# Last output projection of an attention/mLSTM step: one pass per half of the tokens, the norm weight in the last product, Ln from PSUM, and instruction orders stated anew

## The chip, the core and the metric

The kernel runs on one core of one Trainium2 chip. The metric is the device time of one execution in microseconds (us). Before the change the median of three runs is 1099.15 us (1096.28 to 1099.74). A profile of one further execution, which took 1096.84 us, gives the durations used below; its span from the first to the last instruction is 1095.1 us.

The core has five instruction streams: PE (TensorE, matrix products and transposes), DVE (VectorE), ACT (ScalarE), POOL (GpSimd) and SP (SyncE, which here issues most DMAs). Each works through its own list in order; between the lists there are semaphores, so an instruction whose input is not ready holds up all that stand behind it in its list.

## The reference

One inference step of two layers, for 512 tokens of a prompt and 8 sample tokens (520 columns in all), model width 1024, in float32:

```python
x = x + NSA(rmsnorm(x, w_norm0))      # layer 0: native sparse attention, out = W_o(mix * silu(z))
x = x + mLSTM(rmsnorm(x, w_norm1))    # layer 1: matrix-memory LSTM,      out = W_out(h * silu(z))
y = rmsnorm(x, w_norm2)               # final norm, returned for prompt and samples

def rmsnorm(x, w):
    y = x * rsqrt(mean(x * x, axis=-1) + 1e-6)
    return y * w
```

Besides `y` the step returns the new cache rows, the conv rows and the mLSTM's states: per sample a 512 x 512 matrix `C` for each of 4 heads, which are read from HBM, updated and written back.

## The kernel before

**Layout.** `x` is held transposed: 8 tiles of 128 features by 520 tokens. The tokens are worked on in two halves of `CH` = 260 columns (`c` = 0, 1). Every product of the projections is split into three products of a faster 32-bit format: a weight tile `wraw` (128x1024, in the mLSTM's output projection 128x512) is loaded by SP, rounded to `whi` (a Copy on ACT), and its rest `wlo = wraw - whi` is taken on POOL or DVE (`load_w`, L591). PE then adds `hi*whi + lo*whi + hi*wlo`. The activations have the same two parts (`hhi`, `hlo` for the normed input, `uh`, `ul` for the gated output of the mLSTM heads).

**Order.** Nearly every instruction is recorded as a piece and issued later, so all of them carry the line of the recorder's `call` (L487; L498 after the change). Each stage is a list of pieces, and a table of numbers says in which order the pieces are issued. The stages in order of time: `CALLS0` (first norm, key/value projection, compressed cache blocks; to about 215 us), `CALLS2` (q projection, L1381; from about 215 us), `ORDER0` (attention, a planner's operations, `Plan.run` L338), `CALLS1` (attention's output projection, middle norm, the mLSTM's conv and input projection), `ORDER1` (z projection and first states, to about 785 us), `ORDER2` (the four mLSTM heads, the 64 state tiles `cs` of 512 KB, and the output projection of heads 0 to 2; 785 to about 1055 us) and `CALLS3` (output projection of head 3, final norm, `o_y`). A table `MOVED0` or `MOVED1` names pieces that go to another engine than the one written in the code (`swapped`, L466: a Copy of ACT becomes a CAST on DVE, a DVE operation one of POOL and the other way round). `CALLS2` and `CALLS3` have no such table.

**The tail (L2658 to L2682).** For head 3 there are 8 feature tiles `ft`, each with two halves `c`. Before, they are written in the order of `OUT_ORDER`: four tiles in half 0, the same four in half 1, then the other four. One product of a tile and a half is 12 matmuls (4 slices of `uh`/`ul` by 3). The result is added to `x` on DVE; ACT squares it (`sq`); the squares of tiles 0 to 6 are added up in `sacc` (on DVE or POOL), that of tile 7 goes straight to PE, where a product with `ones` sums over the features: two matmuls per half, `sacc` and `sq`. ACT also multiplies every tile by the norm weight `nw` (`x<-x,nw`). Then `rms_factor` (L625): DVE makes `rv = s/1024 + eps` from PSUM, `rsqrt_into` (L609) takes Ln and Exp of it on ACT and one Newton step on DVE, which gives `rr`; each tile is multiplied by `rr` (tiles 1 and 3, `POOLK`, on POOL, the rest on DVE) and stored by SP, for half 1 the odd tiles by ACT.

**Weights of the tail.** Tiles 0 and 1 use buffers of the pool that the heads used; tiles 2 to 7 use a pool `fn` which is opened in the memory that the heads give back, with `W3B` = (raw, hi, lo) buffers. Only two raw tiles of it are under way at a time.

Of the kernel before, what the change touches and what calls it, by code (L numbers as in the profile page):

```python
# [18 lines left out]
CH = 260  # L19
# [34 lines left out]
W3B = (2, 5, 5)  # L54
W3F = 2
OUT_ORDER = [(4 * a + k, c) for a in range(2) for c in range(2) for k in range(4)]
# [253 lines left out]
class Plan:  # L310
# [27 lines left out]
    def run(self, order):  # L338
        assert sorted(order) == list(range(len(self.ops)))
        gone = set()  # L340
        for k in order:
            fn, deps = self.ops[k]
            assert deps <= gone, k
            gone.add(k)
            fn()


class _Now:

# [2442 lines left out]
```

## Time and profile before

| | value |
|---|---|
| median of three runs | 1099.15 us |
| profiled execution / its span | 1096.84 / 1095.1 us |
| mean granted TensorE clock | 0.983 |
| busy: PE, DVE, ACT, POOL | 1048.4, 794.3, 593.0, 270.4 us |
| matmuls | 8563 |
| moved by DMA | 197.18 MB, 180 GB/s on the mean |

A row of the timeline gives start and duration in us, engine, operation, output tile and inputs, shape, and in brackets how long the engine had been idle before it and what it waited for. PE's busy time includes matmuls that run at half clock, so a high share does not say that PE works at its best speed: the column PEclk of the views by windows gives the clock that was granted.

### The profile page before, as it was taken

The numbers are of one execution on the slowest core, as the hardware profiler recorded it, in microseconds if no ns is written. First come the engines' busy times: TensorE is split into PE (matmuls) and PEld (weight loads), VectorE is DVE, ScalarE is ACT, GpSimd is POOL, SyncE is SP. The second block draws the span as 40 slices with busy tenths as digits, with TensorE's granted clock in tenths as the row PEclk, the third lists the DMA queues.
The fourth block names the chain that finished last, engine by engine and source line by source line (L and its number), as shares of the span: only waits on it lengthen the run. The fifth ranks groups of instructions, "written<-read, shape, count | busy, mean of one in ns | idle before, by whom it ended". The sixth has DMA issues, their size and how long they took to land. (4 is left out here: it accounts for less than half of the span.)

```text
span 1095.1 us, 23951 instructions
## 1 busy us (share of the span) xinstructions
PE 1048.4 (96%) x8563; PEld 928.0 (85%) x8563; DVE 794.3 (73%) x1985; ACT 593.0 (54%) x1346; POOL 270.4 (25%) x289
## 2 busy tenths in 40 slices
PE   6999999899999999999999999999989999999986
PEld 5999999699988877879999997898767588777885
DVE  6766844458559999875888785666566878776786
ACT  5343344533467777762443553767566765654535
POOL 1134142133220100102334231421131322412211
PEclk8999999899999999999999998999999999999998
DMA  6554534032423713366542352787877898879443
GB/s 207 179 170 158 186 122 147 19 130 101 141 87 132 199 64 112 114 201 223 182 164 89 136 177 62 285 270 250 265 283 259 267 340 258 300 244 298 148 133 97
DMA packets 124793, 197.18 MB, mean 180 GB/s; under 512 B 16117, under 2 KB 66166, under 8 KB 124418
## 3 DMA queue, kind: packets, MB, share of 16 engines
q1 hardware_dynamic: 118194, 185.58, 51.3%
q10 hardware_dynamic: 6480, 10.08, 2.6%
q8 instruction: 67, 1.10, 0.4%
q14 instruction: 52, 0.43, 0.1%
HBM read 145.89 MB, written 58.10 MB: 186 GB/s over the span
## 5 line engine op out<-in xcount | busy, mean ns | idle before, releaser
L487 PE MATMUL mm<-hhi,whi 128*128 128x260 f32 (+1 forms) x976 | 284.2, 291 | 3.1 <-ACT whi L487 1.6
L487 PE MATMUL mm<-hlo,whi 128*128 128x260 f32 (+1 forms) x976 | 279.4, 286 | 1.8 <-DVE hlo L487 1.8
L487 PE MATMUL mm<-hhi,wlo 128*128 128x260 f32 (+1 forms) x976 | 279.3, 286 | 1.8 <-POOL wlo L487 1.6
L487 PEld LDWEIGHTS mm<-hhi,whi 128*128 128x128 f32 (+1 forms) x976 | 186.0, 191 | 10.8 <-issue 4.2
L487 PEld LDWEIGHTS mm<-hhi,wlo 128*128 128x128 f32 (+1 forms) x976 | 186.0, 191 | 2.4 <-POOL wlo L487 1.9
L487 PEld LDWEIGHTS mm<-hlo,whi 128*128 128x128 f32 (+1 forms) x976 | 185.8, 190 | 2.6 <-DVE hlo L487 2.0
L487 POOL TENSOR_TENSOR wlo<-wraw,whi 128x1024 fp32r<-128x1024 f32 (+1 forms) x54 | 110.8, 2053 | 294.4 <-ACT whi L487 200.7
L487 ACT ACTIVATE whi<-wraw 128x1024 fp32r<-128x1024 f32 (+1 forms) x90 | 79.8, 891 | 64.1 <-PE mm L487 31.5
L487 DVE SCALAR_TENSOR_TENSOR cs<-t,wk,cs 128x512 f32<-128x512 f32 x128 | 89.0, 743 | 14.4 <-ACT cpt L487 5.1
L487 ACT ACTIVATE s<-s,mn 128x256 f32<-128x256 f32 (+3 forms) x128 | 70.8, 555 | 12.6 <-DVE mn L487 12.0
L487 PE MATMUL s<-plo,w1h 128*128 128x256 f32 (+1 forms) x256 | 74.8, 292 | 1.6 <-DVE plo L487 1.5
L487 PE MATMUL s<-phi,w1h 128*128 128x256 f32 (+1 forms) x256 | 76.1, 297 | 0.1
L487 ACT ACTIVATE cs<-cs,SBC 128x1024 f32<-128x1024 f32 x64 | 71.3, 1140 | 8.9 <-PE d L487 8.9
L487 PE MATMUL s<-phi,w1l 128*128 128x256 f32 (+1 forms) x256 | 74.3, 290 | 0.5 <-DVE w1l L487 0.5
L487 PE MATMUL mm<-uh,whi 128*128 128x260 f32 x224 | 66.8, 298 | 2.8 <-DVE x L487 1.9
L487 PE MATMUL mm<-uh,wlo 128*128 128x260 f32 x224 | 64.0, 286 | 0.4 <-POOL wlo L487 0.4
L487 PE MATMUL mm<-ul,whi 128*128 128x260 f32 x224 | 63.9, 285 | 0.0
L487 DVE CUSTOM_DVE_ANT_0 s<-s,D 128x384 f32<-128x384 f32 (+3 forms) x128 | 60.0, 486 | 4.3 <-PE s L487 2.6
L487 DVE TENSOR_TENSOR wlo<-wraw,whi 128x1024 fp32r<-128x1024 f32 (+2 forms) x48 | 50.8, 1063 | 10.8 <-ACT whi L487 9.0
L487 PEld LDWEIGHTS mm<-uh,whi 128*128 128x128 f32 x224 | 42.7, 191 | 10.7 <-DVE x L487 3.2
L487 PEld LDWEIGHTS s<-plo,w1h 128*128 128x128 f32 x256 | 48.6, 190 | 2.9 <-DVE plo L487 2.7
L487 PE MATMUL s<-KA,qst 128*128 128x384 f32 (+3 forms) x128 | 48.1, 382 | 2.2 <-DVE mn L487 1.1
(428 smaller groups left out, 2584.7 us busy)
## 6 DMA issues: line engine op xcount, KB each, us to landing
cs<-in_state_C SPq DMA_DIRECT2D x64, 512.0 KB, 5.7
o_cs<-cs SPq DMA_DIRECT2D x64, 512.0 KB, 4.5
praw<-in_cache SPq DMA_DIRECT2D x128, 128.0 KB, 2.3
dk<-in_cache SPq DMA_DIRECT2D x128, 128.0 KB, 2.3
wraw<-in_m_in SPq DMA_DIRECT2D x32, 512.0 KB, 3.4
wraw<-in_m_out SPq DMA_DIRECT2D x32, 256.0 KB, 3.3
wraw<-in_w_kv SPq DMA_DIRECT2D x11, 512.0 KB, 4.4
wraw<-in_w_q SPq DMA_DIRECT2D x8, 512.0 KB, 3.6
```

Source lines behind the costliest of these rows:

```text
L487: return f(*[real(x) for x in a], **{n: real(x) for n, x in k.items()})
```

## The change

Five edits go together:

1. The tail runs over the halves outside and the tiles inside: all of half 0's tiles are written ahead of half 1's. Each weight tile is loaded and split once, in the pass of half 0, and kept (`W3B` from (2, 5, 5) to (2, 6, 6)).
2. The squares of tiles 6 and 7 both go straight to PE, so a half's sum is three matmuls with `ones` instead of two, and `sacc` takes one square less.
3. The norm weight is the scalar of the last product (`x * nw * rr` in one instruction on DVE); only tiles 1 and 3 keep the scaling on ACT and a plain product.
4. In the middle and the final norm Ln reads the sum in PSUM, with the scale 1/1024 and a bias `eps` from a new constant column. `rv` is still made for the Newton step. The first norm keeps the old way (`cold=True`).
5. All order tables are stated anew (`CALLS0` to `CALLS3`, `ORDER0` to `ORDER2`), and there are tables `MOVED2` for the q projection (29 pieces) and `MOVED3` for the tail (17 pieces).

```diff
-W3B = (2, 5, 5)
+W3B = (2, 6, 6)
-OUT_ORDER = [(4 * a + k, c) for a in range(2) for c in range(2) for k in range(4)]
...
-    912, 17, 0, 14, 8, 9, 18, 10, 11, 15, 19, 34, 12, 43, 16, 35, 37, 13, 20, 36, 60, 913, 44, 30, 45, 38, 31,
+    912, 8, 14, 17, 9, 15, 11, 18, 16, 34, 950, 12, 19, 37, 10, 35, 60, 13, 38, 43, 0, 20, 44, 913, 1, 45, 40,
...
+MOVED3 = (2, 12, 27, 30, 35, 37, 44, 52, 65, 69, 85, 90, 94, 99, 103, 120, 124,)
...
         def call(*a, **k):
             if self.rec.on:
                 return self.rec.add(self.name, m, a, k)
+            if self.rec.flip is not None:
+                engines, self.rec.flip = self.rec.flip, None
+                return swapped(engines, self.name, m, [real(x) for x in a], k)
...
+    parts["eps"] = np.full((128, 1), EPS)
...
-    def rsqrt_into(out, v, pool, shape, tag):
+    def rsqrt_into(out, v, pool, shape, tag, src=None):
...
-        S.activation(y, v, AF.Ln)
+        if src is None:
+            S.activation(y, v, AF.Ln)
+        else:
+            S.activation(y, src, AF.Ln, scale=1.0 / 1024, bias=C("eps"))
...
-    R.run(NE, CALLS2)
+    R.run(NE, CALLS2, MOVED2)
...
-    for ft, c in OUT_ORDER:
-        if ft not in w3:
-            w3[ft] = out_w(3, ft) if ft < W3F else out_w(3, ft, fn, W3B)
-        out_part(3, ft, c, w3[ft], mmb() if (ft + c) % 2 else sb())
+    for c in range(2):
         cs = slice(c * CH, (c + 1) * CH)
-        x = x2[ft]
-        if ft < 7:
-            rms_acc(sacc[c], ft == 0, x[:, cs], fn)
-        else:
+        for ft in range(8):
+            if not c:
+                w3[ft] = out_w(3, ft) if ft < W3F else out_w(3, ft, fn, W3B)
+            out_part(3, ft, c, w3[ft], mmb() if ft % 2 else sb())
+            x = x2[ft]
+            if ft < 6:
+                rms_acc(sacc[c], ft == 0, x[:, cs], fn)
+                if ft in POOLK:
+                    S.activation(x[:, cs], x[:, cs], AF.Copy, scale=nw[:, 2, ft:ft + 1])
+                continue
             sq = fn.tile([128, CH], F32, name="sq", tag="sq")
             S.activation(sq, x[:, cs], AF.Square)
-            pss[c] = sb()
-            PE.matmul(pss[c][:, :CH], ones, sacc[c], start=True, stop=False)
-            PE.matmul(pss[c][:, :CH], ones, sq, start=False, stop=True)
-        S.activation(x[:, cs], x[:, cs], AF.Copy, scale=nw[:, 2, ft:ft + 1])
-    for c in range(2):
-        cs = slice(c * CH, (c + 1) * CH)
+            if ft == 6:
+                pss[c] = sb()
+                PE.matmul(pss[c][:, :CH], ones, sacc[c], start=True, stop=False)
+            PE.matmul(pss[c][:, :CH], ones, sq, start=False, stop=ft == 7)
         r = rms_factor(pss[c], fn)
         for kt in range(8):
-            (G if kt in POOLK else V).tensor_mul(x2[kt][:, cs], x2[kt][:, cs], r)
+            if kt in POOLK:
+                G.tensor_mul(x2[kt][:, cs], x2[kt][:, cs], r)
+            else:
+                V.scalar_tensor_tensor(x2[kt][:, cs], x2[kt][:, cs], nw[:, 2, kt:kt + 1], r, op0=OP.mult, op1=OP.mult)
             (S if c and kt % 2 else SP).dma_start(ap["o_y"][:, kt, cs], x2[kt][:, cs])
-    R.run(NE, CALLS3)
+    R.run(NE, CALLS3, MOVED3)
```

The diff shows a line of the tables only; what they move is seen in the lists of the engines. `MOVED3` puts the POOL products of tiles 1 and 3 by `rr` back on DVE, the rounding `whi` of the tail's tiles 4, 5 and 6 from ACT to DVE, tile 0's `wlo` to POOL and tile 7's to DVE, and three of half 0's and all five of half 1's additions to `sacc` to POOL. Over the whole program DVE has 11 CASTs to `whi` more (8 of 128x1024, 3 of 128x512), ACT as many fewer; 8 of the 16 products `ZS<-ZS,zsg` of the q stage go from DVE to POOL.

**First place: from the key/value stage to the q projection (about 213 to 223 us).** ACT's list before: `VCS<-t` copies transposed value rows out of PSUM, `whi<-wraw` rounds the first two weight tiles of the q projection, and `qst` belongs to its results.

```order
L487 ACTIVATE VC<-t 32x128 x2
L487 ACTIVATE VT_2707<-t 64x2x64
L487 ACTIVATE VCS<-t 128x4x128 x2
L487 ACTIVATE whi<-wraw 128x1024 x2
L487 ACTIVATE qst<-qr 64x252 x2
```

DVE's list at the same place after the change:

```order
L498 COPY VT_2798<-t 64x2x64
L498 CAST KQ<-kct 64x32
L498 TENSOR_TENSOR KQ<-kct,KQ 64x32
L498 CAST whi<-wraw 128x1024
L498 TENSOR_TENSOR wlo<-wraw,whi 128x1024
L498 CAST whi<-wraw 128x1024
L498 TENSOR_TENSOR qr<-mm,rr_694 128x260
```

Both roundings and the first `wlo` have moved from ACT and POOL to DVE, where before the product `qr<-mm,rr` followed the last `KQ` and `VT` rows at once; ACT's two rows `whi` are gone, and POOL keeps the second `wlo`. PE's list there is as it was.

**Second place: from the z projection to the heads (about 783 to 803 us).** PE's list before; `d<-cs,QZ` reads freshly loaded state tiles, `t` and `s` rows are small products of the first head, `mm<-vh,kwh` and its fellows are the state updates:

```order
L487 MATMUL t<-pr,ones 128x64
L487 MATMUL t<-pr,ones 128x32
L487 MATMUL mm<-CT_10302,bdm 128x512
L487 MATMUL mm<-CT_10088,bdm 128x512
L487 MATMUL t<-cst,VS 8x128 x4
L487 MATMUL d<-cs,QZ_10435 32x512 x8
L487 MATMUL t<-bdk,ctw 128x128 x4
L487 MATMUL s<-q,CT_10088 128x512
...
L487 MATMUL t<-VB,OH 128x512
L487 MATMUL d<-cs,QZ_10435 32x512 x4
L487 MATMUL t<-bdk,ctw 128x128 x4
```

PE's list there after the change:

```order
L498 MATMUL t<-pr,ones 128x64
L498 MATMUL t<-cst,lse 128x128 x4
L498 MATMUL t<-pr,ones 128x32
L498 MATMUL mm<-CT_10045,bdm 128x512
...
L498 MATMUL t<-VB,OH 128x512
L498 MATMUL s<-q,CT_10173 128x512
...
L498 MATMUL mm<-CT_10210,bdm 128x512
L498 MATMUL mm<-vh,kwh 128x512
L498 MATMUL mm<-vl,kwh 128x512
L498 MATMUL mm<-vh,kwl 128x512
...
L498 MATMUL t<-VB,OH 128x512
L498 MATMUL d<-cs,QZ_10376 32x512 x4
```

Ahead of the third group `d<-cs,QZ` PE now has a second set of `s<-q,CT` (4 matmuls) and the first state step's twelve matmuls (4 times `vh,kwh`, `vl,kwh`, `vh,kwl`), which came behind it before; and the four `t<-cst,lse`, which came ahead of both `t<-pr,ones`, stand between them.

**Third place: the last head (about 1036 to 1060 us).** ACT's list before; `uh` rows make the last head's activations, and the four `whi` belong to head 2's last tiles:

```order
L487 ACTIVATE whi<-wraw 128x512 x2
L487 ACTIVATE uh_15559<-num 128x512
L487 ACTIVATE whi<-wraw 128x512
L487 ACTIVATE uh_15621<-num 128x512
L487 ACTIVATE whi<-wraw 128x512
L487 ACTIVATE uh_15665<-num 128x512
L487 ACTIVATE uh_15684<-num 128x512
```

ACT's list there after the change:

```order
L498 ACTIVATE whi<-wraw 128x512 x2
L498 ACTIVATE uh_15555<-num 128x512
L498 ACTIVATE rs_y<-hf_v 128x8
L498 ACTIVATE rs_y<-rs_y 128x8
L498 ACTIVATE whi<-wraw 128x512 x2
L498 ACTIVATE uh_15629<-num 128x512
L498 ACTIVATE uh_15666<-num 128x512
L498 ACTIVATE uh_15683<-num 128x512
```

The last rounding of head 2's weights, which stood behind the second `uh`, now stands ahead of it. In the tail behind, the products of the two halves are not strictly one after the other in PE's list: by tile and half they come as 0/0, 1/0, 2/0, 0/1, 3/0, 4/0, 5/0, 6/0, 2/1, 7/0, 1/1, then half 0's sum, then 5/1, 3/1, 4/1, 6/1, 7/1 and half 1's sum; before it was in groups of four tiles.

More of the change, by code (lines that the diff above doesn't have):

```diff
@@ L299 @@
 )
+MOVED2 = (4, 8, 9, 27, 65, 66, 84, 122, 142, 160, 161, 177, 185, 198, 210, 212, 213, 225, 227, 243, 249, 274, 280,
+    283, 289, 320, 326, 333, 347,)
+MOVED3 = (2, 12, 27, 30, 35, 37, 44, 52, 65, 69, 85, 90, 94, 99, 103, 120, 124,)
+MOVEDP0 = ()
+MOVEDP1 = ()
+MOVEDP2 = ()
 KSC = float(np.float32(512.0 ** -0.5))
@@ L336, in op, with run @@
         self.ops.append((fn, deps))
-    def run(self, order):
+    def run(self, order, rec, engines, swap=()):
         assert sorted(order) == list(range(len(self.ops)))
@@ L344, in run @@
             gone.add(k)
+            if k in swap:
+                rec.flip = engines
             fn()
+            assert rec.flip is None
 class _Now:
@@ L412, in __init__ @@
     def __init__(self):
-        self.on, self.pieces, self.label, self.open = False, [], (), None
+        self.on, self.pieces, self.label, self.open, self.flip = False, [], (), None, None
     def at(self, *label):
@@ L623, in rms_acc, with rms_factor @@
             V.tensor_add(acc, acc, sq)
-    def rms_factor(pss, pool, r=None, tag="rv", bufs=1):
+    def rms_factor(pss, pool, r=None, tag="rv", bufs=1, cold=False):
         v = pool.tile([128, CH], F32, name="rv", tag=tag, bufs=bufs)
@@ L629, in rms_factor @@
             r = pool.tile([128, CH], F32, name="rr", tag="rr", bufs=2)
-        rsqrt_into(r, v, pool, [128, CH], "rs")
+        rsqrt_into(r, v, pool, [128, CH], "rs", None if cold else pss[:, :CH])
         return r
@@ L945, in step_kernel @@
             PE.matmul(pss[:, :CH], ones, acc, start=True, stop=True)
-        rms_factor(pss, cw, rr[c], tag="hsg", bufs=2)
+        rms_factor(pss, cw, rr[c], tag="hsg", bufs=2, cold=True)
     R.at("w1", 0)
@@ L1573, in step_kernel @@
     P.LAT, P.SELF = 0.24, 0.07
-    P.run(ORDER0)
+    P.run(ORDER0, R, NE, MOVEDP0)
     actx.close()
@@ L2258, in step_kernel @@
         D["cs", n].users.append(-1)
-    P.run(ORDER1)
+    P.run(ORDER1, R, NE, MOVEDP1)
     r1.close()
@@ L2651, in step_kernel @@
     P.op("SP", 0.4, at, lambda: SP.dma_start(ap["o_np"], nP), r=[("nP", h) for h in range(4)], mb=0.01)
-    P.run(ORDER2)
+    P.run(ORDER2, R, NE, MOVEDP2)
     kctx.close()
```

410 rows, old and new, of tables (CALLS0, CALLS1, CALLS2, CALLS3) are left out of this document.

## The prediction

> **What bounds the kernel now.** I read the page's busy times first, then the wait list of the engine that they point to, then windows of 16 to 20 us where its busy share falls.
>
> ```profile
> PE 1048.4 (96%) x8563; PEld 928.0 (85%) x8563; DVE 794.3 (73%) x1985; ACT 593.0 (54%) x1346; POOL 270.4 (25%) x289
> PE s L487 <- ACT sq L487: 6.0, 2, 5.3
> PE t L487 <- DVE pr L487: 2.0, 1, 2.0
> 200.00:220.00 20.00, 14.82 (x92) 12.19 (x91) 8.04 (x25) 10.95 (x33) 4.23 (x4) 0.80 0.01 4
> 780.00:800.00 20.00, 13.82 (x90) 8.81 (x88) 13.06 (x48) 11.68 (x23) 5.71 (x11) 0.98 0.92 315
> 1040.00:1060.00 20.00, 16.65 (x116) 15.30 (x116) 17.66 (x40) 5.78 (x13) 5.41 (x4) 0.91 0.52 164
> 1080.00:1096.00 16.00, 5.21 (x36) 4.19 (x34) 10.38 (x25) 6.17 (x15) 3.35 (x4) 0.79 0.39 133
> ```
>
> PE is busy for 1048.4 of 1095.1 us. The change removes no product, so it can win back only parts of the 46.7 us in which PE stands still, and of the stretches in which PE runs at half clock. Of a window's row I use the busy time of PE (the second number) and the granted clock (third from the end). The four windows hold 5.2, 6.2, 3.4 and 10.8 us of idle PE, 25.6 of the 46.7, and PE's longer waits fall in them (2.0 us for `pr` in the second; the others stand as rows below), except the 5.3 us for `sq` at the start, where `x` must first be loaded. What the new orders do elsewhere, in attention above all, I can't tell from the lists: PE has no long wait there to remove, and I put it at 0, with 2 us to either side.
>
> **Place 1, start of the q projection: -2.8 us.**
>
> ```profile
> 212.69 2.05 PE L487 MATMUL t<-cst,VT 128*128 128x128 f32 x8 [0.40 <-DVE VC L487]
> 216.37 0.59 PE L487 MATMUL mm<-hhi,whi 128*128 128x260 f32 x1 [1.63 <-ACT whi L487]
> 218.80 0.58 PE L487 MATMUL mm<-hhi,wlo 128*128 128x260 f32 x1 [1.63 <-POOL wlo L487]
> 215.27 1.99 ACT L487 ACTIVATE whi<-wraw 128x1024 fp32r<-128x1024 f32 x2
> 212.77 0.28 DVE L487 COPY VT<-t 64x128 f32<-64x128 f32 x1
> 216.40 4.67 POOL L487 TENSOR_TENSOR wlo<-wraw,whi 128x1024 fp32r<-128x1024 f32 x2 [2.94 <-ACT whi L487]
> L487 DVE CAST whi<-wraw 128x1024 fp32r<-128x1024 f32 (+1 forms) x12 | 8.2, 680 | 7.4 <-PE mm L487 4.3 <-issue 3.1
> L487 DVE TENSOR_TENSOR wlo<-wraw,whi 128x1024 fp32r<-128x1024 f32 (+2 forms) x48 | 50.8, 1063 | 10.8 <-ACT whi L487 9.0 <-issue 1.6
> ```
>
> PE's transposes end at 212.69 + 2.05 = 214.74. Then it waits 1.63 us for `whi`, which ACT can't begin before its copies `VCS` are done (215.27), and 1.63 us for `wlo`, since POOL takes 4.67 / 2 = 2.3 us for one: 3.26 us in all. DVE does nothing after 212.77 + 0.28 = 213.05. After the change it makes the pair there: 213.05 + 0.68 + 1.06 = 214.79, just as PE arrives. The second `whi` ends 0.68 later, at 215.5, and POOL's `wlo` at 217.8; PE needs that pair after the 24 matmuls of the first. So nearly all 3.26 us go. I take 2.8, for half a microsecond of semaphores and of DVE's new rows around `KQ`. Bounds: 1 (the weight tile or the `VT` copy comes later than now) to 3.3.
>
> **Place 2, first state steps: -3.0 us.**
>
> ```profile
> 798.87 1.80 PE L487 MATMUL d<-cs,QZ 128*32 128x512 f32 x8 [3.54 <-DMA cs<-in_state_C]
> 792.77 2.32 PE L487 MATMUL s<-q,CT 128*128 128x512 f32 x8
> 790.36 0.37 SPq L487 DMA_DIRECT2D ab<-rd  x1
> 790.82 0.94 SPq L487 DMA_DIRECT2D cs<-in_state_C  x2
> 795.95 0.69 DVE L487 TENSOR_TENSOR kwl<-t,kwh 128x512 fp32r<-128x512 f32 x1 [0.34 <-ACT kwh L487]
> 796.56 2.20 DVE L487 TENSOR_TENSOR vl<-VT,vh 128x512 fp32r<-128x512 f32 x2
> ```
>
> The state tiles that `d<-cs,QZ` reads at 798.87 were issued at 790.82 behind `ab<-rd`, and took to 798.8, 8 us. In the new list the second `s<-q,CT` (4 rows of the list, 2.32 us in the trace) and the first step's twelve products (0.23 us each, if 512 columns take twice as long as the 0.12 us of 260 in place 3's first row: 2.8 us) come first. Together 5.1 us stand where the wait of 3.54 us was, so that goes; the `lse` products between the two `t<-pr` products cover about 0.5 us of the 2.00. But those twelve products are now themselves early: the third of them wants `kwl`. It ended at 796.64, and in the new list one more `vl` stands ahead of it on DVE (2.20 / 2 = 1.1): 797.7. PE came to the wait at 798.87 - 3.54 = 795.33; 0.5 us less at `pr`, then the second `s<-q,CT` and two products bring it there at 797.6. That is a tie, with the row of DVE not known to half a microsecond; I take **a new wait** of 1.0 us, behind which the twelve products and the next `d` stand. Sum -3.5 - 0.5 + 1.0 = -3.0. Bounds: -4.5 (no new wait, more of `pr` covered) to -1 (`kwl` 2 us later still).
>
> **Place 3, the last head: -1.5 us.**
>
> ```profile
> 1065.51 1.44 PE s L487 x12
> 1049.53 0.36 PE L487 MATMUL mm<-uh,whi 128*128 128x260 f32 x1 [1.08 <-DVE x L487]
> 1047.31 0.63 ACT L487 ACTIVATE uh<-num 128x512 fp32r<-128x512 f32 x1 [1.67 <-DVE num L487]
> 1048.41 0.63 ACT L487 ACTIVATE whi<-wraw 128x512 fp32r<-128x512 f32 x1 [0.47 <-PE mm L487]
> 1055.35 0.69 DVE L487 TENSOR_TENSOR num<-num,zs 128x512 f32<-128x512 f32 x1
> 1056.50 0.80 SPq L487 DMA_DIRECT2D wraw<-in_m_out  x2
> DMA to landing us min/median/max: 3.0/3.1/3.3
> ```
>
> ACT's `whi` at 1048.41 stands behind a `uh` that waited 1.67 us; PE pays 1.08 us and, for the `wlo` behind it, 0.4 more. That goes, but the last head's products still need all `uh` and `ul`, so only what is early on DVE counts: the last `num<-num,zs` now stands ahead of the two additions to `x` that held it till 1055.35, and comes 1 to 1.5 us sooner. It also frees the memory in which tiles 2 and 3 of the tail are loaded, now issued at 1056.50. That chain I follow through: load at about 1055, 3.1 us to landing, `whi` 0.63 and `wlo` 0.69 (half of the 128x1024 rows above give 0.34 to 0.53), so a raw buffer turns over in some 4.4 us. Tiles 4 and 6 are then ready at 1063.8 and 1068.2 or a little earlier. One product of 12 matmuls is 1.44 us (first row, of the chain that ended last); with a start at 1057 PE wants them at 1064.2 and 1067. The end of the last product follows at about 1082.3, against 1083.8 now. Bounds: 0 (every turn as late as now) to -3 (weights never wait). The CASTs of 128x512 are in no row; between 0.34 (half the large one) and 0.68 (the large one) they change this by 0.3 at most per turn.
>
> **Place 4, after the last product: -1.5, and the third sum: +0.4.**
>
> ```profile
> 1085.97 0.42 ACT L487 ACTIVATE rs_y<-rv 128x260 f32<-128x260 f32 x1 [0.86 <-DVE rv L487]
> 1085.51 0.43 DVE L487 TENSOR_SCALAR rv<-s 128x260 f32<-128x260 f32 x1 [0.23 <-PE s L487]
> 1085.86 0.76 DVE L487 TENSOR_TENSOR x<-x,rr 128x260 f32<-128x260 f32 x2
> 1087.81 0.43 DVE L487 SCALAR_TENSOR_TENSOR rr<-rs_t,rs_y 128x260 f32<-128x260 f32 x1
> 1088.62 1.30 DVE L487 TENSOR_TENSOR x<-x,rr 128x260 f32<-128x260 f32 x2
> 1088.31 0.97 POOL L487 TENSOR_TENSOR x<-x,rr 128x260 f32<-128x260 f32 x1 [2.38 <-DVE rr L487]
> 1090.30 0.89 POOL L487 TENSOR_TENSOR x<-x,rr 128x260 f32<-128x260 f32 x1 [1.01 <-ACT x L487]
> 1091.21 1.33 ACTq L487 DMA_DIRECT2D o_y<-x  x3
> L487 POOL TENSOR_TENSOR sacc<-sacc,sq 128x260 f32<-128x260 f32 x10 | 10.2, 1022 | 21.8 <-ACT sq L487 21.7
> ```
>
> Ln no longer waits for `rv`: 1085.97 becomes 1085.51, and `rr` ends at 1087.78 instead of 1088.24 (-0.46). Then DVE has 8 products and no POOL beside it. Two take 0.76 us where POOL rests (1085.86) and 1.30 while POOL multiplies (1088.62); seven steps of 0.34 and a last one of 0.42 end at 1090.6. ACT's last three stores, which now wait for POOL's product (1090.30 + 0.89) and end at 1092.54, are then spread out, and the last ends near 1091.0: -1.5. That DVE's new product with two operands and a scalar costs the same is read off `rr`, 0.43. Half 0's third matmul with `ones` lies on PE's path: it runs twice over 260 columns, 0.22 us each: +0.4. Half 1's runs in the shadow of the last `sq`. Half 1's additions to `sacc` on POOL take 1.02 us each; the last begins two products (2.9 us) before the end plus about 0.9 for add and square, and is done about 0.9 us before PE's last product: no cost. Bounds for the place: -2 to 0.
>
> [...]
>
> **Sum.** -2.8 - 3.0 - 1.5 - 1.5 + 0.4 = -8.4 us. On the profiled execution (1096.84) that is 1088.4; the median of the runs, 1099.15, lies 2.3 above it, and I carry the difference over: 1090.8.
>
> **Rivals.**
>
> *More than that, the clock as well.*
>
> ```profile
> 212.00:217.00 5.00, 2.97 (x11) 1.93 (x10) 0.66 (x3) 3.40 (x7) 1.12 (x2) 0.50 0.01 3
> 217.00:222.00 5.00, 3.37 (x15) 3.20 (x15) 0.00 (x0) 0.27 (x1) 4.07 (x2) 0.50 0.28 105
> 799.00:802.00 3.00, 3.00 (x14) 1.43 (x11) 2.48 (x4) 2.35 (x3) 0.02 (x1) 0.51 0.84 323
> ```
>
> At 212 to 222 and again right after the hole at 799 the granted clock is half. If a filled hole also keeps the clock up, 5 us at 217 and 3 us at 799 run twice as fast: up to another 2.5 + 1.5 us, 1086.8. Against it at the first place: the clock was down from 212 on, before the hole. [...]
>
> [...]
>
> *Slower.* One mechanism can outweigh all: the state tiles in the stretch from 800 to 1034, where DMA is near full. SP's queue is in order, and a load that stands behind a store waits till the store's tile is done. In the new list 22 of the 64 loads of `cs` stand behind one to three stores more than before, 12 behind fewer. The one such wait in the trace costs 3.54 us. From four uncovered waits of that size the kernel is slower: -8.4 + 4 x 3.54 = +5.8, 1104.9. For it: the DMA share of 0.92 at 780 to 800 and 8 us to landing. Against it: most stand behind one store more only, and PE shows one such wait in the 64 loads of before.
>
> **How the numbers follow.** About 0.3% (3.3 us) is what a measurement of this kernel tells from no change. Forecast 0.46 (1090.8; all bounds of its terms at once, the 2 us of the rest too, 1084.7 to 1099.6), more 0.20 (1087), given back 0.20 (1097, on both sides of the bound, counted as no change), slower 0.14 (1105). Hence faster 0.66, same 0.20, slower 0.14. The range from 1084 to 1102 leaves out the slower case and the far end of the best, together somewhat under 0.2.
>
> **What will show it.** Place 1 is right if PE waits under 0.5 us at its first `mm<-hhi,whi` and `wlo` after the transposes, and DVE's CASTs stand ahead of them. Place 2: no `d<-cs` wait over 1 us before the second step, and a wait for `kwl` of about 1.5. Place 3: no wait for POOL's `wlo` in head 2's last tiles, first `fn` loads at about 1055 less what was won before. Place 4: 8 DVE products in about 2.8 us, last store 1.1 to 1.6 us sooner after the last product. It is wrong if PE's idle time over 800 to 1034 grows by more than 4 us, or if the waits at places 1 to 3 come back under other names.

## The result, and the profile after

The changed kernel takes 1090.05 us (median of 8 runs, 1087.04 to 1092.11), the kernel before 1099.38 us in the same series (8 runs, 1093.96 to 1101.85). The ratio is 0.9919, with an interval of 0.9898 to 0.9941: 9.3 us, or 0.8%, faster. The forecast was 1090.8.

The profiled execution took 1091.77 us (span 1089.9, mean clock 0.986). It lies high among its kernel's runs, as that of before (1096.84) lies low among its own; the two profiles are therefore only 5.2 us of span apart where the medians are 9.3 apart.

The page of the changed kernel: busy times, then PE's waits (total, times, longest):

```profile
PE 1044.1 (96%) x8567; PEld 927.1 (85%) x8567; DVE 792.9 (73%) x1981; ACT 578.4 (53%) x1324; POOL 276.6 (25%) x301
PE mm L498 <- DVE hlo L498: 4.1, 2, 3.3
PE mm L498 <- DVE x L498: 3.3, 4, 1.4
PE mm L498 <- DVE kvt L498: 3.2, 2, 2.7
PE t L498 <- DVE pr L498: 1.8, 1, 1.8
PE s L498 <- POOL sacc L498: 0.6, 1, 0.6
```

The waits for `hlo` and `kvt` lie in the first stage, and they are new at this size. Windows of the changed kernel (start:end, length, busy time of PE, PEld, DVE, ACT, POOL with counts, granted clock, DMA share, GB/s):

```profile
20.00:40.00 20.00, 16.19 (x119) 15.74 (x120) 17.91 (x26) 2.74 (x8) 8.99 (x5) 0.91 0.34 104
120.00:140.00 20.00, 17.33 (x130) 17.21 (x130) 15.70 (x29) 4.09 (x16) 1.21 (x2) 0.91 0.46 152
785.00:1020.00 235.00, 232.13 (x1380) 174.57 (x1380) 179.50 (x389) 144.07 (x242) 69.08 (x87) 0.99 0.82 277
```

The same windows of the kernel before:

```profile
20.00:40.00 20.00, 18.95 (x137) 18.19 (x136) 15.67 (x33) 4.04 (x11) 3.20 (x2) 0.89 0.46 152
120.00:140.00 20.00, 20.00 (x165) 19.89 (x164) 16.11 (x27) 7.51 (x23) 3.25 (x3) 1.00 0.59 199
785.00:1020.00 235.00, 227.63 (x1333) 169.16 (x1333) 176.80 (x380) 140.19 (x234) 65.90 (x85) 0.99 0.82 275
```

PE loses 2.8 and 2.7 us in the first two and gains 4.5 in the heads. The milestones of the two timelines give the account by stage (worked out from the starts and ends of PE's rows):

| stretch on PE | before | after | difference |
|---|---|---|---|
| start to the transposes of `VT` | 212.69 | 222.56 | +9.9 |
| those to the first q product | 3.68 | 1.60 | -2.1 |
| q, attention, projections, heads, to the end of the last `d<-cs` | 802.0 | 788.0 | -14.0 |
| to the end of the last product of head 3 | 65.4 | 65.9 | +0.5 |
| to the end | 11.3 | 11.8 | +0.4 |

So the total came out as forecast from parts that did not: a large loss in the first stage, a larger gain in the long middle, and nothing from the tail. The third and the fourth row hold stretches of half clock too, which do not fall at the same places in the two profiles (last section).

### The profile page after: what moved, and what is told of

It reads as the page before. It is cut to its first block, busy times and chain, and to the rows that moved or that the text cites. A ratio compares the mean times of both kernels' runs of the same rounds, so it can differ in the third digit from the quotient of the medians.

```text
span 1089.9 us, 23970 instructions
## 1 busy us (share of the span) xinstructions
PE 1044.1 (96%) x8567; PEld 927.1 (85%) x8567; DVE 792.9 (73%) x1981; ACT 578.4 (53%) x1324; POOL 276.6 (25%) x301
## 4 chain that ended last, share of the span: by engine, by line
PE 75%; DVE 11%; ACT 5%; issue 3%; DMA 3%; SPq 2%; POOL 0%; POOLq 0%; DVEq 0%; ACTq 0%
PE mm L498 48%; PE s L498 15%; PE t L498 7%; PE d L498 5%; ACT s L498 2%; DVE s L498 2%; SPq L498 2%; DVE wlo L498 1%; DVE x L498 1%; DMA praw<-in_cache 1%; DMA wraw<-in_m_out 1%; DVE qst L498 1%; DVE sm L498 1%; ACT pt L498 1%; DMA wraw<-in_w_kv 1%
## 5 line engine op out<-in xcount | busy, mean ns | idle before, releaser
L498 PE MATMUL mm<-hhi,whi 128*128 128x260 f32 x976 | 282.4, 289 | 4.6 <-DVE kvt L498 3.2
L498 PE MATMUL mm<-hlo,whi 128*128 128x260 f32 x976 | 277.9, 285 | 4.1 <-DVE hlo L498 4.1
L498 PE MATMUL mm<-hhi,wlo 128*128 128x260 f32 x976 | 278.5, 285 | 2.0 <-DVE wlo L498 1.6
L498 PEld LDWEIGHTS mm<-hhi,whi 128*128 128x128 f32 x976 | 184.9, 189 | 10.1 <-DVE kvt L498 3.7
L498 PEld LDWEIGHTS mm<-hlo,whi 128*128 128x128 f32 x976 | 184.6, 189 | 5.0 <-DVE hlo L498 4.5
L498 PEld LDWEIGHTS mm<-hhi,wlo 128*128 128x128 f32 x976 | 184.8, 189 | 2.9 <-DVE wlo L498 2.3
L498 POOL TENSOR_TENSOR wlo<-wraw,whi 128x1024 fp32r<-128x1024 f32 (+1 forms) x50 | 104.0, 2080 | 257.9 <-ACT whi L498 192.8
L498 ACT ACTIVATE whi<-wraw 128x1024 fp32r<-128x1024 f32 (+1 forms) x79 | 69.8, 886 | 81.0 <-PE mm L498 61.9
L498 ACT ACTIVATE s<-s,mn 128x384 f32<-128x384 f32 (+3 forms) x128 | 70.7, 555 | 15.9 <-DVE mn L498 15.7
L498 PEld LDWEIGHTS s<-phi,w1h 128*128 128x128 f32 x256 | 48.9, 191 | 2.9 <-ACT phi L498 2.5
```

The lines of the kernel that those rows point to most:

```text
L498: return f(*[real(x) for x in a], **{n: real(x) for n, x in k.items()})
```

## The experiments

Each kernel is made of the kernel before with one part of the change, or of the changed kernel with one part undone. The change's tables are independent lists, so they can be exchanged one by one; the diffs show a line or a part of one. The middle norm's Ln from PSUM is in none of the parts and was not measured by itself. Ratios are against the kernel before, run beside; a gain in us below is worked out from the ratio. The median of the kernel before was 1099.4 us beside the changed kernel, 1098.4 beside the next eight, 1097.7 beside the last four, two of which (Ln first, two sums on DVE) ran once only.

| kernel | median us | ratio, interval |
|---|---|---|
| changed | 1090.05 | 0.9919 [0.9898, 0.9941] |
| changed, first stage's list of before | 1082.9 | 0.9864 [0.9845, 0.9883] |
| changed, `KB` cleared early | 1086.6 | 0.9898 [0.9876, 0.9919] |
| before + q projection's list | 1095.0 | 0.9971 [0.9955, 0.9986] |
| before + tail | 1097.95 | 0.9994 [0.9976, 1.0012] |
| before + heads' lists | 1090.05 | 0.9917 [0.9891, 0.9942] |
| before + attention's and its projections' lists | 1092.8 | 0.9948 [0.9929, 0.9968] |
| first stage of before and `KB` early (C1 below) | 1081.7 | 0.9850 [0.9820, 0.9880] |
| changed, products of tiles 1 and 3 on POOL | 1091.85 | 0.9940 [0.9911, 0.9968] |
| C1, tile 6 ahead of tile 7 | 1082.8 | 0.9868 [0.9849, 0.9886] |
| C1, tile 6 first, Ln first, two sums on DVE | 1083.4 | 0.9871 [0.9852, 0.9889] |

### The first stage

```diff
-    7, 0, 2, 12, 1, 10, 9, 6, 29, 25, 124, 35, 26, 30, 23, 36, 31, 8, 24, 11, 61, 32, 177, 33, 131, 27, 62, 34,
+    7, 0, 1, 12, 8, 2, 134, 10, 9, 6, 29, 25, 27, 26, 30, 35, 28, 129, 31, 36, 15, 32, 33, 11, 16, 177, 72, 34,
...
```

> The changed kernel with the order of the first stage (CALLS0) as it was before; all else changed. In the changed kernel's profile the first stage ends 9.9 us later than before (the transposes of VT start at 222.56 instead of 212.69), with 7.2 us more idle PE. Theory: that is a real loss of the new order, which the gains behind it outweigh. Then this kernel is 7 to 10 us faster than the changed one, about 1082, and the transposes start at 211 to 214. Rival: the late start costs nothing, because later stages are held by transfers or by the clock anyway. Then it stays at 1088 to 1091.

1082.9 us. With the list `CALLS0` of before, and all else of the change kept, the kernel gains another 7 us (7.2 by the medians, 6 by the ratios), and the two intervals do not meet. The transposes of `VT` begin at 213.18. The new order of the first stage costs this much, and the other edits together are worth 15 us.

Where it costs it is seen at PE's two longest new waits. The timeline of the changed kernel, first around 20 us:

```profile
24.92 0.59 PE L498 MATMUL mm<-hlo,whi 128*128 128x260 f32 x1 [3.29 <-DVE hlo L498]
20.13 4.34 DVE L498 CAST w1h<-wraw 128x1024 fp32r<-128x1024 f32 x1
20.42 3.51 POOL L498 MEMSET KB<- 128x4096 f32 x1
...
122.68 0.39 PE L498 MATMUL mm<-hhi,whi 128*128 128x260 f32 x1 [2.67 <-DVE kvt L498]
120.22 0.69 DVE L498 CAST phi<-praw 128x1024 fp32r<-128x1024 f32 x1 [4.88 <-issue]
122.20 0.43 DVE L498 TENSOR_TENSOR kvt<-mm,rr 128x260 f32<-128x260 f32 x1
```

A CAST of 128x1024 takes 0.69 us in the fifth row and 4.34 in the second, where it ends 0.54 us after a MEMSET on POOL of 3.51 us (20.42 + 3.51 = 23.93). The `hlo` that PE needs stands behind it on DVE. The next kernel moves the MEMSET alone, to right behind the one that makes `ones`:

```diff
-    7, 0, 2, 12, 1, 10, 9, 6, 29,
+    7, 0, 3, 2, 12, 1, 10, 9, 6, 29,
...
-    184, 3, 57,
+    184, 57,
```

> The changed kernel with one piece of the first stage moved: POOL's MEMSET of KB (128x4096, 3.51 us at 20.42) is issued right behind that of ones, at about 1 us, when DVE has nothing to do. Theory: the MEMSET stalls DVE's CAST w1h, which took 4.34 us from 20.13 instead of about 0.7, and through hlo behind it PE (3.29 us of waiting). Then the CAST takes under 1 us, PE's wait goes, and the kernel is 2.5 to 4 us faster than the changed one, about 1087. Rival: the CAST is long because its weight tile (load issued at 13.96) landed late. Then it is as long as before and the time stays at 1089 to 1091.

The same CAST in the timeline of this kernel:

```profile
20.78 0.89 DVE L496 CAST w1h<-wraw 128x1024 fp32r<-128x1024 f32 x1
```

0.89 us instead of 4.34, and PE's wait for `hlo` is 0.8 instead of 3.3. The median is 3.4 us lower (2.3 by the ratios); the intervals of the two ratios overlap, so the total alone would not show it, but the two rows do. Before the change the same MEMSET stood at 62.73, where it met a CAST of 128x256 (2.87 us at 63.53, where the next one takes 0.29); PE then waited 1.3 us at most for the `plo` behind it.

In both pairs of rows the CAST ends just behind the MEMSET: 0.15 us behind in the kernel before (63.53 + 2.87 = 66.40, 62.73 + 3.52 = 66.25), 0.54 us in the changed one. In the pair of before the MEMSET came first (62.73, 63.53); in that of the changed kernel the CAST began, by the trace, 0.29 us ahead of it (20.13, 20.42) and still ended behind it. What makes the CAST last so long beside the MEMSET is not shown.

For the second wait, at 122.68, the timeline says only this much: DVE stood still for 4.88 us ahead of the CAST `phi<-praw`, whose pages come by DMA, and `kvt` stood behind it. The row names no releaser. That the pages came late through the new order of loads is an inference (loads of `praw` were issued until 117.34 and took 2.2 to 3.6 us to land) and was not tried by itself.

Both remedies in one kernel, C1: the first stage's list of before with the early MEMSET.

> The changed kernel with the first stage's old order and in it the MEMSET of KB at the start, as in the run that moves it alone. In the profile of before that MEMSET ran at 62.73 for 3.52 us, and a CAST phi beside it took 2.87 us from 63.53, after which PE waited 1.26 us for plo. Theory: 1 to 2 us less than the changed kernel with the old first stage, about 1080.5. Rival: PE's wait there has another cause: no difference to that kernel.

1081.7 us, ratio 0.985. Against the list of before alone (1082.9) no difference is shown; of that kernel's waits on PE, the one of 0.76 us for `plo` at 67.67 is gone. C1 beats both kernels of this case, 1.5% under the one before, with an interval that doesn't meet that of the changed one, and is the base of the last four kernels.

### The q projection alone

```diff
-    7, 26, 0, 8, 27, 9, 16, 28, 64, 45, 263, 261, 193, 10, 17, 20, 18, 256, 24, 22, 19, 23, 29, 11, 14, 12, 15,
+    45, 7, 8, 0, 9, 16, 26, 191, 189, 188, 195, 27, 10, 28, 17, 257, 20, 18, 193, 24, 164, 190, 29, 11, 12, 64,
...
-    R.run(NE, CALLS2)
+    R.run(NE, CALLS2, MOVED2)
```

> The kernel before with the new order of the q projection (CALLS2 and MOVED2) alone: place 1 of the prediction. Theory: both waits of 1.63 us go and nothing takes their place: -2.8 us, 1096.6. Rival 1: the filled hole also keeps the clock up (10.2 us at half clock from 212): -4 to -6 us. Rival 2: the gain is given back in the q projection: 0.

1095.0 us, -3.2, with 12 runs on this side. DVE makes the first pair at 212.97 (CAST 0.92, then `wlo` 1.23), and of PE's two waits of 1.63 us one of 0.75 is left. The window of this kernel, and then that of before:

```profile
212.00:222.00 10.00, 8.10 (x61) 7.23 (x61) 6.12 (x10) 1.99 (x5) 3.12 (x3) 1.00 0.32 106
```

```profile
212.00:222.00 10.00, 6.34 (x25) 5.13 (x25) 0.66 (x3) 3.67 (x7) 5.20 (x3) 0.50 0.15 54
```

61 matmuls instead of 25: the clock is whole as well. That it goes with the list is seen in the other kernels that keep the old list of the q projection, those with the tail, the heads and the attention alone:

```profile
212.00:222.00 10.00, 6.25 (x25) 4.93 (x26) 0.75 (x4) 3.89 (x7) 5.20 (x3) 0.53 0.16 54
212.00:222.00 10.00, 6.44 (x27) 5.53 (x28) 0.62 (x3) 3.36 (x5) 5.20 (x3) 0.51 0.22 63
212.00:222.00 10.00, 6.08 (x27) 4.78 (x27) 0.71 (x4) 3.85 (x7) 5.20 (x3) 0.61 0.18 57
```

All four profiles with the old list have 10.2 us at half clock between 211 and 225; of the ten with the new list eight have one stretch of 3.4 us there and two have none. So the gain at this place is not that of the two waits alone. Over 30 us, before and then with the new list:

```profile
212.00:242.00 30.00, 26.34 (x190) 25.13 (x190) 12.17 (x33) 11.52 (x22) 10.64 (x7) 0.83 0.30 102
212.00:242.00 30.00, 27.41 (x219) 26.33 (x219) 22.68 (x47) 8.35 (x19) 7.39 (x8) 1.00 0.35 112
```

PE stands still for 1.1 us less (new waits farther on take back part of the 2.5 us won at the two) and issues 29 matmuls more, at 0.12 us each 3.5 us of work. Some 2.4 us of the gain at this place are therefore clock.

### The heads alone

The lists `ORDER1` and `ORDER2`; the first line of the second:

```diff
-    303, 290, 291, 292, 306, 294, 2, 402, 288, 1, 286, 284, 5, 13, 295, 341, 21, 3, 22, 293, 585, 342, 305, 296,
+    291, 290, 292, 593, 294, 303, 306, 286, 341, 288, 21, 32, 1, 408, 22, 295, 342, 5, 0, 13, 307, 293, 2, 10,
...
```

> The kernel before with the new orders from the z projection to the end of head 2's products (ORDER1 and ORDER2) alone: place 2, and the heads' share of place 3. Theory: the 3.54 us wait for state tiles goes and no like wait comes elsewhere in the heads: -3 us by place 2, up to -4.5 with the end of the heads, 1095 to 1096.5. Rival: the boundary's gain is lost in waits for state tiles between 800 and 1034: 0 or slower. In the changed kernel's profile PE's idle time from the first to the last read of the state tiles is 2.7 us against 5.8 before.

1090.05 us, -9.1: the largest part of the change, as large as the whole. The windows of this kernel over the heads, and over the hole of 3.54 us that the prediction spoke of:

```profile
785.00:1020.00 235.00, 232.24 (x1381) 174.55 (x1381) 179.56 (x390) 144.37 (x242) 69.06 (x87) 0.99 0.82 278
797.00:803.00 6.00, 6.00 (x26) 4.20 (x25) 4.94 (x8) 3.32 (x5) 0.88 (x3) 1.00 0.71 267
```

The second window of the kernel before:

```profile
797.00:803.00 6.00, 4.13 (x19) 2.47 (x20) 4.48 (x6) 5.35 (x6) 2.02 (x3) 0.72 0.92 348
```

In the heads 4.6 us of idle PE are gone (232.24 - 227.63), more than the 3.54 of the one long wait: five short waits of 0.3 to 0.6 us went too, and one of 0.8 is new. At 797 to 803 the clock, 0.72 before, is whole; 0.72 over 6 us is some 3.4 us at half clock (6 times twice the missing 0.28). But this profile has a stretch of the same length earlier, and over 785 to 1020 the clock is 0.99 in both, so these two profiles show no gain by the clock:

```profile
788.00:792.00 4.00, 3.97 (x10) 1.42 (x14) 2.83 (x17) 2.80 (x8) 1.63 (x3) 0.57 0.93 344
```

That leaves some 4.5 us of the 9.1 that I can't place. The two profiles themselves are 6.6 us of span apart (1095.1 and 1088.5).

### Attention and the projections behind it

The lists `ORDER0` and `CALLS1`, with Ln in the middle norm as before; the first line of `ORDER0`:

```diff
-    912, 17, 0, 14, 8, 9, 18, 10, 11, 15, 19, 34, 12, 43, 16, 35, 37, 13, 20, 36, 60, 913, 44, 30, 45, 38, 31,
+    912, 8, 14, 17, 9, 15, 11, 18, 16, 34, 950, 12, 19, 37, 10, 35, 60, 13, 38, 43, 0, 20, 44, 913, 1, 45, 40,
...
```

> The kernel before with the new orders of attention, its output projection and the mLSTM's input part (ORDER0 and CALLS1) alone; the prediction put them at 0, with 2 us to either side. In the changed kernel's profile the stretch from attention's last score product to the lse transposes is 4.9 us shorter than before, and before had 6.8 us at half clock there (669 to 676) that the changed one has not. Theory: the filled hole at 666.84 (0.98 us) keeps the clock up: -3.4 to -5 us, 1094 to 1096. Rival: the prediction's 0, since the low clock comes and goes from run to run.

1092.8 us, -5.7, where the prediction had 0 with 2 to either side. Its profile is that of its slowest run (1096.03), so it can't show all of the gain. What it shows is one place of the kernel before, in windows of 4 us:

```profile
664.00:668.00 4.00, 3.02 (x46) 2.02 (x38) 2.09 (x11) 0.00 (x0) 2.68 (x8) 1.00 0.00 0
668.00:672.00 4.00, 3.79 (x23) 3.73 (x24) 1.06 (x8) 1.25 (x7) 0.00 (x0) 0.67 0.00 0
672.00:676.00 4.00, 4.00 (x20) 4.00 (x20) 1.62 (x11) 0.97 (x4) 0.00 (x0) 0.50 0.04 2
```

and of the new lists:

```profile
665.00:675.00 10.00, 9.79 (x104) 8.18 (x96) 5.80 (x32) 4.09 (x14) 2.54 (x8) 1.00 0.15 46
```

Before the change PE ran some 6.8 us at half clock there, behind 0.98 us of idle time (4.00 - 3.02), and is nearly all busy in the rows. Half clock shows as busy time (4.00 of 4 us at a clock of 0.50 in the third row), so a stage can hold a gain although PE has no wait to remove. The place moves: the kernel with the q projection's list alone has the attention lists of before, and its clock is whole here and half for 6.8 us from 405 on. The amount follows the lists: between 350 and 700 the four profiles with the attention lists of before have 6.8 to 10.2 us at half clock, the ten with the new lists 3.4 or none. At least 3.4 us less at half clock are up to 1.7 us of time, an estimate (half of it); how the rest of the 5.7 us divides isn't settled.

### The tail alone

The rewritten tail with `CALLS3` and `MOVED3`; the middle norm's Ln stays as before.

```diff
-    for ft, c in OUT_ORDER:
+    for c in range(2):
...
+        for ft in range(8):
...
-    R.run(NE, CALLS3)
+    R.run(NE, CALLS3, MOVED3)
```

> The kernel before with the rewritten tail alone (two passes over the halves, norm weight in the last product, Ln from PSUM in the last norm, CALLS3 and MOVED3); all other orders as before, and the middle norm's Ln from rv. Theory: places 3 and 4 are the tail's own: -1.5 - 1.1 = -2.6 us, 1096.8. Rival: place 3 comes from the new order of the heads (ORDER2), where the whi and uh rows are, and the tail brings only place 4: about -1 us. Second rival: with the weights needed sooner and the heads' end as before, the weights come late: 0 or slower.

1097.95 us: no difference that 12 runs can show (-2.6 to +1.3 us by the interval). In its profile 11.8 us lie between the end of the last product and the end, as in the changed kernel, against 11.3 before. Why, the timeline of the changed kernel says, DVE, ACT, POOL and PE behind the last product:

```profile
1080.37 0.43 DVE L498 TENSOR_SCALAR rv<-s 128x260 f32<-128x260 f32 x1 [0.59 <-PE s L498]
1080.84 0.48 ACT L498 ACTIVATE rs_y<-s,cst 128x260 f32<-128x260 f32 x1 [1.69 <-DVE rv L498]
1083.60 2.48 DVE L498 SCALAR_TENSOR_TENSOR x<-x,nw,rr 128x260 f32<-128x260 f32 x6
1077.07 1.62 POOL L498 TENSOR_TENSOR sacc<-sacc,sq 128x260 f32<-128x260 f32 x2 [0.33 <-ACT sq L498]
1078.75 0.71 PE L498 MATMUL s<-sacc,ones 128*128 128x260 f32 x2 [0.63 <-POOL sacc L498]
```

Ln reads `s` from PSUM as the edit says (second row) and still begins only when DVE's `rv`, which reads the same `s`, is done. Six products with the scalar take 2.48 us, 0.41 each; the two plain ones at their sides keep a step of 0.34. POOL's last addition ends at 1078.69, and PE waits 0.63 us for it. The next kernels take these apart.

The products of tiles 1 and 3 by `rr` back on POOL, as before the change:

```diff
-MOVED3 = (2, 12, 27, 30, 35, 37, 44, 52, 65, 69, 85, 90, 94, 99, 103, 120, 124,)
+MOVED3 = (2, 12, 27, 30, 35, 37, 44, 52, 85, 90, 94, 99, 103)
```

> The changed kernel with the products of tiles 1 and 3 by rr left on POOL, in both halves (four pieces taken out of MOVED3): the part of place 4 that comes from moving them to DVE. Theory: the last DVE products are again stretched (about 1.3 us for two where POOL works, 0.76 where it rests) and the last stores wait for POOL: 0.5 to 1 us slower than the changed kernel between the last product and the end (11.75 us there now, 12.2 to 12.8 then). Rival: all of place 4 is Ln reading PSUM and the norm weight; then no difference.

1091.85 us; the interval overlaps that of the changed kernel, so the verdict is the profile's: 13.1 us from the last product to the end instead of 11.8. Its rows, DVE and POOL side by side, PE waiting for POOL, and one of half 0's products on POOL:

```profile
1081.72 3.44 DVE L498 SCALAR_TENSOR_TENSOR x<-x,nw,rr 128x260 f32<-128x260 f32 x6
1081.83 1.85 POOL L498 TENSOR_TENSOR x<-x,rr 128x260 f32<-128x260 f32 x2 [4.60 <-DVE rr L498]
1077.29 0.71 PE L498 MATMUL s<-sacc,ones 128*128 128x260 f32 x2 [1.51 <-POOL sacc L498]
1075.62 0.73 POOL L498 TENSOR_TENSOR x<-x,rr 128x260 f32<-128x260 f32 x1
```

Beside POOL the six products take 3.44 us instead of 2.48. Taking POOL out of the end is worth 1.4 us within the new tail, but 0.9 of that is PE's wait for `sacc` (1.51 instead of 0.63): with the new tail half 1's additions are on POOL, and half 0's product (last row) stands ahead of the last of them. Behind `rr` the difference is 0.5 us (7.2 us to the end, 6.75 in the changed kernel). The other edits of the tail lose more than the 1.4 (11.3 us before the change).

Ln ahead of `rv` in the tail's list (C1 as base):

```diff
-56, 100, 57, 58, 88, 59,
+56, 100, 58, 57, 88, 59,
...
-64, 112, 113, 68,
+64, 113, 112, 68,
```

> The kernel with the first stage's old order and the early MEMSET (the run before this one that has both), and in the tail's list Ln ahead of rv, in both halves. In the changed kernel ACT's Ln still waits for DVE's rv (1.69 us idle, rv 1080.37 + 0.43, Ln at 1080.84), though it reads PSUM itself; its wait is on DVE. Theory: only the order of the two holds Ln, since two readers of one PSUM tile are made to follow each other; with Ln first it starts right behind the sum, and from the last product to the end it takes 0.4 to 0.5 us less (11.7 now, 11.2 to 11.3 then). Rival: ACT and DVE really can't read the tile at the same time and rv then comes late for the Newton step: no difference.

1079.62 us in one run, beside C1's 1080.71 to 1084.99. The rows of this kernel:

```profile
1068.85 0.48 ACT L496 ACTIVATE rs_y<-s,cst 128x260 f32<-128x260 f32 x1 [1.03 <-PE s L496]
1069.36 0.43 DVE L496 TENSOR_SCALAR rv<-s 128x260 f32<-128x260 f32 x1 [0.85 <-ACT rs_y L496]
1070.74 0.43 DVE L496 SCALAR_TENSOR_TENSOR rr<-rs_t,rs_y 128x260 f32<-128x260 f32 x1
```

Now Ln waits for PE's sum itself, and `rv` waits for Ln. From the start of the first reader to the end of `rr` it is 2.32 us (1071.17 - 1068.85); in the changed kernel 2.78 (1083.15 - 1080.37). That is the 0.46 us that the prediction had credited to the edit, and it came with the exchange of two pieces, not with the operand.

The last two additions to `sacc` back on DVE:

```diff
-MOVED3 = (2, 12, 27, 30, 35, 37, 44, 52, 65, 69, 85, 90, 94, 99, 103, 120, 124,)
+MOVED3 = (2, 12, 27, 30, 35, 37, 44, 52, 65, 69, 85, 90, 94, 120, 124)
```

> The same base, with the last two additions to half 1's sacc left on DVE (two pieces taken out of MOVED3). In the changed kernel PE waits 0.63 us for POOL's sacc at 1078.75, and ACT's last squares wait for POOL too (0.62 and 0.46 us). Theory: POOL's additions hold the sum; then from the last product to the end 0.4 to 0.8 us less (11.7 now). Rival: DVE, with two additions more, gives it back ahead of the last addition to x: within 0.2.

1080.2 us in one run. PE's wait for `sacc` falls from 0.63 us (C1) to 0.41, now for DVE, and the stretch behind the last product by 0.2. In the kernel with Ln first, where the additions stay on POOL, that wait is 0.39, so the 0.2 us is not shown to come from this edit; the sum is bound by the squares and DVE's queue nearly as much as by POOL.

### The last head

In the end of `ORDER2`, tile 6 of head 2's output ahead of tile 7, and the additions to `x` earlier:

```diff
-280, 931, 935, 947, 941, 885, 942, 930, 886, 932, 945, 876, 943, 880, 877, 881, 944, 878, 946, 938, 882, 887, 879, 936, 948, 883, 949, 937, 939
+280, 931, 930, 935, 947, 941, 885, 942, 886, 932, 936, 876, 938, 937, 880, 945, 939, 877, 881, 943, 878, 944, 882, 887, 879, 948, 883, 949, 946
```

> The same base, with the end of the heads' list written so that tile 6 of head 2's output projection comes ahead of tile 7, with its additions to x on DVE early. In the changed kernel PE waits 1.39 us at 1044.05 for an addition to x, and the product that waits is of tile 7, whose weights come later than tile 6's. Theory: what holds the end of the heads is the order of DVE's additions to x (they free the PSUM bank), not ACT's whi; then the last head's first product starts 1 to 1.5 us sooner after the last read of the state tiles (40.2 us now), and the kernel is about 1 us faster than its base (1081.7). Rival: the last head's uh and ul set its start whatever the products of head 2 do: no difference in the start, PE only waits later.

1082.8 us, no different from C1. PE's rows in this kernel, and two of DVE and ACT:

```profile
1038.15 0.36 PE L494 MATMUL mm<-uh,whi 128*128 128x260 f32 x1 [0.87 <-DVE x L494]
1043.45 0.39 PE L494 MATMUL s<-uh,whi 128*128 128x260 f32 x1 [1.94 <-ACT whi L494]
1044.96 0.39 PE L494 MATMUL s<-uh,wlo 128*128 128x260 f32 x1 [1.00 <-POOL wlo L494]
1039.65 1.66 DVE L494 TENSOR_TENSOR num<-num,zs 128x512 f32<-128x512 f32 x1
1041.34 1.15 ACT L494 ACTIVATE uh<-num 128x512 fp32r<-128x512 f32 x2 [5.48 <-DVE num L494]
```

The wait for `x` falls from 1.41 us (C1) to 0.87, and the 0.52 behind it is gone; in their place stand 1.94 us for the last head's first `whi` and 1.00 for its `wlo`. Counted from the last read of the state tiles, PE comes to the last head 2.2 us sooner than in C1, but the additions to `x` now stand ahead of the last `num<-num,zs` on DVE, which ends 2.0 us later; ACT's `uh` waits for it (last row), and `whi`, which stands behind `uh`, begins 1.4 us later. The last head's first product moves by 0.2 us only.

All three of these edits in one kernel:

> All three edits together on the same base. If each theory holds, 1.8 to 2.8 us faster than the base, about 1079.5; from the last product to the end about 10.8. If the rivals hold, 1081 to 1082.

1083.4 us, again no better than C1. From the last product to the end it is the shortest of all (10.9 us), but the last product comes later, behind the same two waits (2.0 and 1.0 us).

## Why the forecast was right in total, and where it wasn't

| term | forecast | measured part by part |
|---|---|---|
| first stage | 0 | +7 (6 to 7.2), by undoing it |
| place 1, q projection | -2.8 | -3.2 |
| attention and its projections | 0 | -5.7 |
| places 2 and 3, what lies in the heads' lists | -3.0, and part of -1.5 | -9.1 |
| places 3 and 4 and the third sum, what lies in the tail | the rest of -1.5, -1.5, +0.4 | -0.7, not told from 0 |
| sum | -8.4 | about -12; the kernel itself -9.3 |

The sum of the parts differs from the whole by less than the intervals of five measurements together.

**First stage: wrong.** The step that failed is "PE has no long wait there to remove, and I put it at 0, with 2 us to either side": where no wait can be removed, a new order can still add some. 2.3 to 3.4 us came from one MEMSET that now stands beside a CAST that PE waits for, and shown is also that the list as a whole costs 6 to 7.

**Attention: wrong by the same step.** It brought 5.7 us without a long wait to remove. What the profiles show of it is less half clock, which the wait list does not have; the rest is open.

**Place 1: right about the two waits, its size by luck.** They fell from 3.26 us to 0.20 in the changed kernel and 0.75 in the part alone, and -3.2 lies within the bounds of -1 to -3.3. But the sum had no term for the clock, which brought more at this place than the idle time (an estimate of 2.4 of some 3.5 us), and none for the new waits behind it. The rival "the clock as well" was right here; what the prediction held against it, that the clock was down from 212 on before the hole, was true of some 2.8 of the 10.2 us at half clock only: from 211.00 to 214.74, where the hole begins, the clock is 0.63 on the mean (2 x 0.37 x 3.74 = 2.8 us at half), and from there to 221.60 it is 0.50. The case "given back", 1097, did not come: this place's list alone brought 3.2 us and the heads' lists 9.1.

**Place 2: right about the wait, too small in size.** The wait of 3.54 us for `cs` is gone. The new wait of 1.0 for `kwl` did not come. PE and DVE in the changed kernel:

```profile
800.68 0.40 PE L498 MATMUL mm<-vh,kwl 128*128 128x512 f32 x1
797.72 0.68 DVE L498 TENSOR_TENSOR kwl<-t,kwh 128x512 fp32r<-128x512 f32 x1
```

`kwl` ends at 798.40 and the third product, which reads it first, starts at 800.68: 2.3 us of room, where the forecast saw a tie. Both of its estimates were off. Counted from the second product of `pr` (787.75 here; 785.9 in the forecast) `kwl` is there after 10.7 us, not 11.8, and PE after 12.9, not 11.7; two `mm<-CT,bdm` of 0.5 us together also stand ahead of the twelve products. In C1, whose clock is whole there, the room is 2.0 us. The credit of 0.5 us at `pr` shrank to 0.2 (2.0 to 1.8). Of the rest of the 9.1, some 1 us lies in the short waits of the heads, for which the prediction had no term; the other 4.5 are open. The rival "slower", with four uncovered waits of `cs`, did not happen: idle PE in the heads fell.

**Place 3: wrong.** The prediction put the wait of 1.08 us at 1049.53 down to ACT's `whi`; its own row said `<-DVE x`. After the change it stands as

```profile
1044.05 0.36 PE L498 MATMUL mm<-uh,whi 128*128 128x260 f32 x1 [1.39 <-DVE x L498]
```

with `whi` early. The stretch from the last `d<-cs` to the last product is 0.5 us longer instead of 1.5 shorter. Some 0.3 of that is the third matmul of half 0's sum, which lies in this stretch and which the forecast had at +0.4: the squares' products with `ones` take 1.04 us there instead of 0.71. Clearing the wait for `x` by the order of the additions holds back the last head's `num`, and with it `uh` and `whi`.

**Place 4: wrong.** "Ln no longer waits for `rv`" failed (0.46 us, given back by the order of the two readers), six of the eight products cost 0.41 and not 0.34 (0.4 us together), and half 1's additions, put at "no cost", became 0.63 us of PE's wait. From the end of `rr` to the end of the last store's issue it is 3.8 us instead of 4.3, so 0.5 of the 1.1 us forecast for products and stores came; but the end follows that issue after 2.9 us instead of 2.6, which takes 0.3 back. The additions themselves did not double beside DVE: 1.62 us for two, where the ten on POOL before the change took 1.02 each on the mean and 0.77 at the median. A product on DVE beside them did (0.81 us at 1077.29, where one at 1083.26 takes 0.43). Leaving POOL's products on POOL would have cost the new tail 1.4 us, as seen above, but only 0.5 of that behind `rr`, where the prediction had looked.

The total was right by luck: an unforeseen loss of 7 us and some 2 us that the tail did not bring stood against some 12 us of unforeseen gain in attention and the heads. The range was right by that too, not by its reasons.

## What to carry to other kernels

A stage without long waits of the bottleneck engine is not a stage that a new order leaves alone (here -5.7 us in attention, +7 in the first stage): measure each list by itself and keep those that pay; here three of five did, one showed nothing, and putting the fifth back won another 6 to 7 us. A wait list has no row for half clock: PE counts as busy in it (4.00 of 4 us at a clock of 0.50). Look for GpSimd's long operations beside VectorE's CASTs on the critical path (here a MEMSET of 3.51 us, and a CAST that took 4.34 us beside it and 0.89 without it). Moving the operand of Ln to PSUM removed no wait here while `rv`, another reader of the same tile, stood ahead of it in the program (ACT idle for 1.69 us, `<-DVE rv`); the exchange of the two won 0.46 us.

## What the runs showed of the hardware

The half clock moves between runs, in places that no edit touched. The changed kernel with the first stage's list of before, and C1, share every list and differ in the place of one MEMSET at the very start. Two windows of the first, and then of C1:

```profile
404.00:409.00 5.00, 5.00 (x59) 3.50 (x50) 4.90 (x18) 2.52 (x8) 0.94 (x3) 1.00 0.00 0
664.00:669.00 5.00, 5.00 (x31) 5.00 (x31) 2.28 (x16) 0.97 (x4) 0.00 (x0) 0.66 0.00 0
```

```profile
404.00:409.00 5.00, 5.00 (x35) 3.90 (x27) 4.08 (x15) 1.85 (x7) 0.74 (x2) 0.66 0.00 0
664.00:669.00 5.00, 4.79 (x42) 4.73 (x41) 3.09 (x22) 1.61 (x8) 0.48 (x2) 1.00 0.00 0
```

One execution lost its clock at 664, the other at 405. Each of these two stretches is about 3.4 us long (0.66 on the mean of 5 us is half clock for 2 x 0.34 x 5 = 3.4 us); the one from 212 on in the kernel before, 10 us at 0.50, is about three times as long. The one of C1 followed no hole: PE was busy for 9.69 of the 10 us ahead of 404.

```profile
394.00:404.00 10.00, 9.69 (x111) 7.29 (x112) 9.27 (x44) 7.30 (x24) 0.93 (x2) 1.00 0.10 29
```

One stretch of 3.4 us costs up to 1.7 us, an estimate (half of it); that a few more or fewer of them make the 3 us by which runs of one kernel differ is my reading, not shown. A single profile can therefore not tell a gain of 2 us from the clock. Many can: at the q projection and in attention the fourteen profiles of this case part by their lists, as told above, so there the amount of half clock goes with the order (10.2 us with the old list of the q projection, 3.4 or none with the new; 6.8 to 10.2 us with the attention lists of before, 3.4 or none with the new), and only its place wanders. Why it does is not shown.
